# Stick-breaking heads in four steps: the next head's scan is queued behind the split of this head's turned weights

## The chip, the cores and the metric

The kernel runs on one core of a Trainium2 chip. The core has a matrix engine (TensorE, PE in the profile, with its weight loads shown apart as PEld), a vector engine (VectorE, DVE), an activation engine (ScalarE, ACT), GpSimd (POOL) and SyncE (SP), whose queue issues most of the transfers between the chip's memory and the core's own. Each engine works through its own instructions in the order in which they were written for it. The metric is the time of one execution on the device in microseconds (us), given as the median over the runs.

## The reference

The program is one block of a network on 512 tokens of width 1024: a normalisation and a projection, then two branches (stick-breaking attention with 16 heads of width 64, and a retention with 4 heads), a gated merge, and a feed-forward part. The change concerns only the stick-breaking branch and what is computed beside it:

```python
def stick_breaking_attention(q, k, v):
    ...
    for i in range(s_len // BLOCK):
        ...
        z = jnp.einsum('bhtd,bhsd->bhts', qb, kb).astype(jnp.float32) * scale
        ...
        mask = s_pos[None, :] < t_pos[:, None]
        log_1m_beta = jnp.where(mask, jax.nn.log_sigmoid(-z), 0.0)
        after = lax.cumsum(log_1m_beta, axis=3, reverse=True) - log_1m_beta
        log_a = jax.nn.log_sigmoid(z) + after
        a = jnp.where(mask, jnp.exp(log_a), 0.0)
        outs.append(jnp.einsum('bhts,bhsd->bhtd', a.astype(v.dtype), vb))
```

The merge that follows multiplies each branch by a gate, `sigmoid(br + b_branch)`, where `br` is a further part of the first projection. In the kernel these gates are computed in the same stretch of time as the heads.

## The kernel before

Everything is held transposed, features on the 128 partitions and tokens along the free axis. A float32 matrix product is made of three products of rounded parts: a value is split into a high part (a copy on ScalarE, L208) and a low part (the difference, on VectorE, L210), and one product of eight 128-row blocks is 24 matmuls of 128 x 512 (`gemm`). Weights come in by SP in tiles `raw` (three buffers) and are split into `whi` and `wlo` (four buffers each).

**One head.** `sb_front(h)` computes the scores of head h into three PSUM banks named `z` (8 matmuls, L614), takes two sigmoids of them on ScalarE (L622, eight instructions), and runs on VectorE a product scan from the right over each row (L625, two instructions) and a multiplication (L626, two instructions). What stands then in `b4` and `b1` are the attention weights, with queries on the partitions. `sb_back(h)` turns them: ten transposes on TensorE (L637) write three `z` banks, which are then split into high and low parts (L640 to L643: three copies on ScalarE, three differences on VectorE). With these it forms the output (eight matmuls into the bank `av`, L651), copies it out on ScalarE (L653), moves half of it to the other partitions by a transfer (L655) and adds (L656).

There are only three `z` banks (`BUFS`, L92). So the transposes of head h-1 write banks that the sigmoids of head h have just read, and the scores of head h+1 write banks that the splits of head h-1 have read.

**The order.** `heads(h)` at L1099 emits `sb_front(h)` and then `sb_back(h-1)`: on VectorE the scan of head h stands ahead of the differences of head h-1. Between heads the loop at L1111 places other products: after each even head up to 10 a pair of products `sb_qk(p)` for the queries and keys of two later heads, after each odd head one gate product (`mix(1)`), and after heads 13 and 15 four gate products each. A scheduler then moves the instructions of each engine against each other, by its own estimate of when each can start. It interleaves the transposes and output matmuls with the neighbouring product. In what it made of this, head h = 1, 3, 5, ... has two products ahead of it, and h = 2, 4, 6, ..., 12 has one. Heads 13 and 15 have less than one product between them and the head before.

`tc.issue_after(ins)` adds an ordering edge from the instructions of its block to `ins`, for those on the engine of `ins` only.

Of the kernel before, what the change touches and what calls it, by code (L numbers as in the profile page):

```python
# [117 lines left out]
def kernel(  # L118
# [19 lines left out]
    def nm(s):  # L138
        uid[0] += 1
        return f"{s}_{uid[0]}"  # L140
# [4 lines left out]
    def psa():  # L145
        return pspool.tile([P, S], F32, tag="av", bufs=BUFS["av"], name=nm("av"))

    def psz():
        return pspool.tile([P, S], F32, tag="z", bufs=BUFS["z"], name=nm("z"))

    def pair(tag):
        return apool.tile([P, 2, S], F32R, tag=tag, bufs=BUFS[tag], name=nm(tag))

    def tmp():
        return apool.tile([P, S], F32, tag="t", bufs=BUFS["t"], name=nm("t"))

    def otile():
        return apool.tile([P, S], F32, tag="o", bufs=BUFS["o"], name=nm("o"))
# [4 lines left out]
    def f(ap):  # L163
        return ap.bitcast(F32)
# [41 lines left out]
    def split(dst_hi, dst_lo, src, scale=1.0, eng=None):  # L206

        nc.scalar.activation(dst_hi, src, AF.Copy, scale=scale)  # L208
        if isinstance(scale, float) and scale == 1.0:
            return (eng or nc.vector).tensor_sub(dst_lo, src, f(dst_hi))  # L210
        return nc.vector.scalar_tensor_tensor(
            dst_lo, src, scale, f(dst_hi), op0=ALU.mult, op1=ALU.subtract
        )
# [15 lines left out]
    def mm(o, lhs, rhs, start, stop):  # L229
        return nc.tensor.matmul(o, lhs, rhs, start=start, stop=stop, skip_group_check=True).ins  # L230
# [99 lines left out]
    def sigmoid_tables():  # L330
        return tc.keep_in_program_order(nc.scalar.preload_act_table_set("sigmoid_and_others"))

    def ln_exp_tables():
        return tc.keep_in_program_order(
            nc.scalar.preload_act_table_set("natural_log_exp_and_others")
        )
# [222 lines left out]
    sbq, sbk, sbv = {}, {}, {}  # L559
# [16 lines left out]
    def sb_qk(p):  # L576
        qp, kp = ps(), ps()
        gemm(qp, weight(("sq", p)), hs)
        gemm(kp, weight(("sk", p)), hs)
        sb_qk_store(p, qp, kp)  # L580
# [27 lines left out]
    def sb_front(h):  # L608
        q, k = sbq[h], sbk[h]
        z = [psz(), psz(), psz()]  # L610
        for i, bank, c, _ in reversed(SEG):
            w = (i + 1) * P
            for n in range(2):
                head_pe[h] = mm(z[bank][:, c : c + w], q[:, n, i * P : (i + 1) * P], k[:, 0:w],  # L614
                                n == 0 and c == 0, n == 1)
        n4, n1, b4, b1 = stick_sets[h % 2]
        for segs in ((3,), (2, 0), (1,)):
            for (t4, t1), scale in (((n4, n1), -1.0), ((b4, b1), 1.0)):
                for i, bank, c, at in (SEG[i] for i in segs):
                    w = (i + 1) * P - 1  # L620
                    t = t1 if i == 1 else t4
                    nc.scalar.activation(t[:, at : at + w], z[bank][:, c : c + w], AF.Sigmoid, scale=scale)  # L622
        for n, b, d in ((n4, b4, diag), (n1, b1, diag[:, 640:896])):
            w = n.shape[-1]
            nc.vector.tensor_tensor_scan(n[:, ::-1], n[:, ::-1], d[:, ::-1], 0.0, op0=ALU.mult, op1=ALU.max)  # L625
            nc.vector.tensor_mul(b[:, 0 : w - 1], b[:, 0 : w - 1], n[:, 1:w])  # L626
        return b4, b1

    def sb_back(h, b4, b1):
        vt = sbv[h // 4]  # L630
        at = [psz(), psz(), psz()]
        for i, _, _, a in reversed(SEG):
            t = b1 if i == 1 else b4
            for j in range(i + 1):
                bank, c = TGEO[j]
                c += (i - j) * P
                nc.tensor.transpose(at[bank][:, c : c + P], t[:, a + j * P : a + (j + 1) * P], ident)  # L637
        avs = []
        for bank in range(3):
            w = TBANKW[bank]  # L640
            hl = pair("s")
            split(hl[:, 0, :w], hl[:, 1, :w], at[bank][:, :w])
            avs.append(hl)  # L643
        o = psa()
        r, hf = (h % 4) // 2, h % 2
        for j in (3, 2, 1, 0):
            bank, c = TGEO[j]
            w = S - j * P
            v = vt[j // 2][:, j % 2, r * 256 + hf * P : r * 256 + hf * P + P]
            for i in range(2):  # L650
                mm(o[:, j * P : S], v, avs[bank][:, i, c : c + w], j == 3 and i == 0, j == 0 and i == 1)  # L651
        u, u2 = tmp(), tmp()
        nc.scalar.activation(u, o, AF.Copy)  # L653
        own, oth = (slice(0, HD), slice(HD, P)) if hf == 0 else (slice(HD, P), slice(0, HD))
        nc.sync.dma_start(u2[own], u[oth])  # L655
        nc.vector.tensor_add(o_sb[h // 2][own], u[own], u2[own])  # L656
# [49 lines left out]
    def ret_v(h, first, between):  # L706
        vt = [pair("v") for _ in range(4)]
        for i in range(2):
            if i == 1:
                between()  # L710
            banks = first if i == 0 else [ps(), ps()]
            if i == 1:
                tok_proj(banks, [("rv", h, i, half) for half in range(2)])
            for b in range(4):
                c = slice(i * 256, (i + 1) * 256)
                split(vt[b][:, 0, c], vt[b][:, 1, c],
                      banks[b // 2][:, (b % 2) * 256 : (b % 2) * 256 + 256])
        return vt

    def ret_scores(h, qk):  # L720
        q1, q2, k1, k2 = qk
        z = [psz(), psz(), psz()]
        st = {}
        for j in (3, 2, 1, 0):
            bank, c, t0, w = GEO[j]
            js = slice(j * P, (j + 1) * P)
            for n, (q, k) in enumerate(((q1, k1), (q2, k2))):
                mm3(z[bank][:, c : c + w], k[:, 0, js], k[:, 1, js], q[:, 0, t0:S], q[:, 1, t0:S],
                    n == 0 and j != 2, n == 1)
        for j in (3, 2, 1, 0):  # L730
            bank, c, t0, w = GEO[j]
            if bank not in st:
                st[bank] = pair("s")
            hl = st[bank]
            split(hl[:, 0, c : c + w], hl[:, 1, c : c + w], z[bank][:, c : c + w],
                  gk[:, h * 4 + j : h * 4 + j + 1])
        for bank in (2, 1, 0):
            for i in range(2):
                causal(st[bank][:, i, :], bank)
        return st  # L740
# [317 lines left out]
    vt = ret_v(0, v_ps, lambda: st.update(ret_scores(0, qk)))  # L1058
# [6 lines left out]
    for h in range(3):  # L1065
# [3 lines left out]
        vt = lambda: [rvts[b] for b in range(4)]  # L1069
# [3 lines left out]
    act_table = sigmoid_tables()  # L1073
# [5 lines left out]
    def sb_v(g):  # L1079

        sbv[g] = [pair("v") for _ in PI]
        for n, vt in enumerate(sbv[g]):
            nc.sync.dma_start(f(vt), vspill[2 * (g - 2) + n])

    sbv.update({g: [vts[g, n] for n in PI] for g in PI})
    mixes = [(ret_mix, d) for d in range(8)] + [(sb_mix, d) for d in range(8)]

    def mix(n):
        for _ in range(n):
            fn, d = mixes.pop(0)  # L1090
            fn(d)
# [5 lines left out]
    fronts = {}  # L1097

    def heads(h):  # L1099
        with tc.issue_after(act_table.ins):  # L1100
            if h < 16:
                fronts[h] = sb_front(h)
            if h:
                if h % 8 == 1 and h > 8:
                    sb_v(2)
                    sb_v(3)
                if h % 2:
                    o_sb[h // 2] = otile()
                sb_back(h - 1, *fronts.pop(h - 1))

    for h in range(17):  # L1111
        heads(h)
        p = h // 2 + 2
        if h % 2 == 0 and p < 8:
            sb_qk(p)
        elif h % 2 and mixes:
            mix(1 if p < 8 else len(mixes) if h == 15 else 4)
    ln_exp_tables()
    acts = []
    for j in range(8):  # L1120
        hl = pair("q" if j < 4 else "s")
# [3 lines left out]
    for d in range(8):  # L1125
# [7 lines left out]
        hl = pair("h")  # L1133
        ins = split(hl[:, 0, :], hl[:, 1, :], t)
# [596 lines left out]
```

## Time and profile before

| | us |
|---|---|
| median of 3 runs | 1153.26 |
| lowest and highest run | 1152.96 and 1153.92 |
| profiled execution, its own time | 1152.75 |
| its span, first to last instruction | 1151.0 |

The profile is of that one execution. Its page shows for each engine the busy time and share of the span; other views show stretches of time (windows), single instructions in order of time (the timeline), and who waited for whom (waits). In these, a row's `[x <-ENGINE tile Lnnn]` says that the engine sat idle for x us before that row and what ended the idle time. `x7` at the end of a row means that seven equal instructions are merged into it. Instructions on one engine overlap at their ends, so rows start a little before the row above ends.

The heads lie between 478 and 710 us. The scores of head 1 start at 489.5 us and those of head 13 at 645.6 us.

### The profile page before, as it was taken

The numbers are of one execution on the slowest core, as the hardware profiler recorded it, in microseconds if no ns is written. First come the engines' busy times: TensorE is split into PE (matmuls) and PEld (weight loads), VectorE is DVE, ScalarE is ACT, GpSimd is POOL, SyncE is SP. The second block draws the span as 40 slices with busy tenths as digits, with TensorE's granted clock in tenths as the row PEclk, the third lists the DMA queues.
The fourth block names the chain that finished last, engine by engine and source line by source line (L and its number), as shares of the span: only waits on it lengthen the run. The fifth ranks groups of instructions, "written<-read, shape, count | busy, mean of one in ns | idle before, by whom it ended". The sixth has DMA issues, their size and how long they took to land. (4 is left out here: it accounts for less than half of the span.)

```text
span 1151.0 us, 16148 instructions
## 1 busy us (share of the span) xinstructions
PE 1119.5 (97%) x6196; PEld 965.2 (84%) x6196; DVE 839.5 (73%) x1181; ACT 554.4 (48%) x869; POOL 55.3 (5%) x94
## 2 busy tenths in 40 slices
PE   8999999999999999999999899999999999999996
PEld 7888888888888887877777678889999999999986
DVE  7997756959959867466666754776997776677656
ACT  5445345445445544355555544355744454454333
POOL 0000000111021110000000000000000000000000
PEclk9999999999999999999999999999999999999998
DMA  9724432766777576856565338872546654565322
GB/s 353 271 73 147 139 118 92 221 129 199 238 147 245 149 185 209 225 151 177 151 185 150 109 114 272 276 217 59 138 140 175 179 145 134 151 176 152 90 80 74
DMA packets 63437, 190.93 MB, mean 166 GB/s; under 512 B 7808, under 2 KB 9856, under 8 KB 63360
## 3 DMA queue, kind: packets, MB, share of 16 engines
q1 hardware_dynamic: 56048, 171.02, 46.6%
q0 software_dynamic: 6768, 18.35, 9.4%
q8 instruction: 49, 0.80, 0.3%
q10 hardware_dynamic: 544, 0.52, 0.1%
q14 instruction: 28, 0.23, 0.1%
HBM read 146.35 MB, written 16.78 MB: 142 GB/s over the span
## 5 line engine op out<-in xcount | busy, mean ns | idle before, releaser
L230 PE MATMUL ps<-h,whi 128*128 128x512 f32 (+1 forms) x1154 | 340.3, 376 | 0.2
L230 PEld LDWEIGHTS ps<-h,whi 128*128 128x128 f32 x1154 | 208.0, 189 | 35.1 <-ACT h L435 1.6
L230 PE MATMUL ps<-h,wlo 128*128 128x512 f32 (+1 forms) x577 | 214.6, 376 | 0.0
L210 DVE TENSOR_TENSOR wlo<-raw,whi 128x1024 fp32r<-128x1024 f32 (+1 forms) x106 | 127.3, 1201 | 99.3 <-ACT whi L208 96.6
L208 ACT ACTIVATE whi<-raw 128x1024 fp32r<-128x1024 f32 (+1 forms) x106 | 110.6, 1044 | 162.0 <-PE ps L230 108.5
L230 PE MATMUL ps<-s,whi 128*128 128x512 f32 x480 | 148.5, 390 | 0.0
L230 PEld LDWEIGHTS ps<-h,wlo 128*128 128x128 f32 x577 | 108.9, 189 | 17.4
L230 PE MATMUL z<-q,whi 128*128 128x256 f32 x504 | 106.8, 283 | 0.0
L230 PEld LDWEIGHTS ps<-s,whi 128*128 128x128 f32 x480 | 89.3, 188 | 18.5 <-DVE s L210 0.5
L871 DVE TENSOR_TENSOR wlo<-s,whi 128x1024 fp32r<-128x1024 f32 x46 | 56.2, 1225 | 54.7 <-ACT whi L867 54.7
L230 PE MATMUL ps<-s,wlo 128*128 128x512 f32 x240 | 93.4, 389 | 0.0
L230 PEld LDWEIGHTS z<-q,whi 128*128 128x128 f32 x504 | 84.9, 192 | 1.5
L867 ACT ACTIVATE whi<-s 128x1024 fp32r<-128x1024 f32 x47 | 49.7, 1057 | 58.6 <-PE ps L230 46.0
L230 PE MATMUL ps<-whi,h 128*128 128x512 f32 (+1 forms) x272 | 77.8, 365 | 0.0
L1172 DVE SCALAR_TENSOR_TENSOR o<-ps,mod,o 128x512 f32<-128x512 f32 (+1 forms) x63 | 42.4, 680 | 29.1 <-PE ps L230 29.1
L230 PEld LDWEIGHTS ps<-whi,h 128*128 128x128 f32 x272 | 49.2, 188 | 9.1 <-ACT t L1011 0.6
L230 PEld LDWEIGHTS ps<-s,wlo 128*128 128x128 f32 x240 | 45.1, 188 | 9.4
L867 ACT ACTIVATE whi<-raw 128x1024 fp32r<-128x1024 f32 x28 | 29.6, 1058 | 42.1 <-PE ps L230 40.3
L230 PE MATMUL ps<-wlo,h 128*128 128x512 f32 (+1 forms) x136 | 49.5, 364 | 0.0
L230 PE MATMUL ps<-q,whi 128*128 128x256 f32 (+1 forms) x224 | 49.2, 314 | 0.0
L230 PE MATMUL z<-qp,whi 128*128 128x256 f32 x168 | 47.2, 283 | 0.0
L230 PE MATMUL z<-q,wlo 128*128 128x256 f32 x168 | 46.4, 283 | 0.0
(318 smaller groups left out, 2105.1 us busy)
## 6 DMA issues: line engine op xcount, KB each, us to landing
raw<-wp SPq DMA_DIRECT2D x139, 512.0 KB, 4.1
araw<-wada SPq DMA_DIRECT2D x32, 512.0 KB, 4.0
araw<-wp SPq DMA_DIRECT2D x30, 512.0 KB, 4.7
s<-wp SPq DMA_DIRECT2D x24, 512.0 KB, 5.4
sraw<-wada SPq DMA_DIRECT2D x16, 512.0 KB, 7.4
q<-qp SPq DMA_DIRECT2D x32, 256.0 KB, 3.8
spill<-o POOLq DMA_DIRECT2D x24, 256.0 KB, 4.7
o<-xT SPq DMA_DIRECT2D x16, 256.0 KB, 4.2
```

Source lines behind the costliest of these rows:

```text
L208: nc.scalar.activation(dst_hi, src, AF.Copy, scale=scale)
L210: return (eng or nc.vector).tensor_sub(dst_lo, src, f(dst_hi))
L230: return nc.tensor.matmul(o, lhs, rhs, start=start, stop=stop, skip_group_check=True).ins
L867: nc.scalar.activation(hi, t, AF.Copy)
L871: nc.vector.tensor_sub(lo, t, f(hi))
L1172: return nc.vector.scalar_tensor_tensor(x1[d][:, hv], o[:, hv], mod[:, gcol + d : gcol + d + 1], x1[d][:, hv], op0=ALU.mult, op1=ALU.add,)
```

## The change

`sb_front` now ends with the sigmoids. The scan and the multiplication become `sb_scan`, the transposes and the split `sb_turn`, which also returns the last difference (`ins`), and the output matmuls with what follows become `sb_out`. `heads(h)` emits, in this order: scores and sigmoids of h, transposes and split of h-1, scan of h, output of h-1. The scan of h is put behind the last difference of h-1 on VectorE by `issue_after`. No instruction is added or removed, but for two runs of equal matmuls that now print as one row.

The loop now places two gate products after each of heads 12 to 15, in place of four after 13 and four after 15. Their sequence is unchanged.

```diff
                     nc.scalar.activation(t[:, at : at + w], z[bank][:, c : c + w], AF.Sigmoid, scale=scale)
+        return n4, n1, b4, b1
+
+    def sb_scan(n4, n1, b4, b1):
         for n, b, d in ((n4, b4, diag), (n1, b1, diag[:, 640:896])):
             w = n.shape[-1]
             nc.vector.tensor_tensor_scan(n[:, ::-1], n[:, ::-1], d[:, ::-1], 0.0, op0=ALU.mult, op1=ALU.max)
             nc.vector.tensor_mul(b[:, 0 : w - 1], b[:, 0 : w - 1], n[:, 1:w])
-        return b4, b1
-
-    def sb_back(h, b4, b1):
-        vt = sbv[h // 4]
+
+    def sb_turn(n4, n1, b4, b1):
         at = [psz(), psz(), psz()]
...
-            split(hl[:, 0, :w], hl[:, 1, :w], at[bank][:, :w])
+            ins = split(hl[:, 0, :w], hl[:, 1, :w], at[bank][:, :w])
             avs.append(hl)
+        return avs, ins
+
+    def sb_out(h, avs):
+        vt = sbv[h // 4]
         o = psa()
...
         with tc.issue_after(act_table.ins):
+            ins = act_table
             if h < 16:
                 fronts[h] = sb_front(h)
             if h:
                 if h % 8 == 1 and h > 8:
                     sb_v(2)
                     sb_v(3)
+                avs, ins = sb_turn(*fronts.pop(h - 1))
+            if h < 16:
+                with tc.issue_after(ins.ins):
+                    sb_scan(*fronts[h])
+            if h:
                 if h % 2:
                     o_sb[h // 2] = otile()
-                sb_back(h - 1, *fronts.pop(h - 1))
+                sb_out(h - 1, avs)
 
     for h in range(17):
         heads(h)
         p = h // 2 + 2
-        if h % 2 == 0 and p < 8:
+        if p > 7:
+            mix(min(2, len(mixes)))
+        elif h % 2:
+            mix(1)
+        else:
             sb_qk(p)
-        elif h % 2 and mixes:
-            mix(1 if p < 8 else len(mixes) if h == 15 else 4)
```

On VectorE, around head 1, the order before was the following. `qp` is the split of a key product, the SCALAR_TENSOR_TENSOR rows of L625 are the scans, and `s<-z` at L210 are the three differences of head 0's turned weights.

```order
L210 TENSOR_TENSOR qp_4279<-ps_4217,qp_4279 128x512
L625 SCALAR_TENSOR_TENSOR s_3955<-s_3955,table_3945 128x1024
L625 SCALAR_TENSOR_TENSOR t_3957<-t_3957,table_3945 128x256
L626 TENSOR_TENSOR s_3956<-s_3956,s_3955 128x1023
L626 TENSOR_TENSOR t_3957<-t_3957 128x255
L210 TENSOR_TENSOR s_4332<-z_4319,s_4332 128x512
L210 TENSOR_TENSOR s_4335<-z_4320,s_4335 128x512
L210 TENSOR_TENSOR s_4338<-z_4321,s_4338 128x256
L210 TENSOR_TENSOR wlo_4593<-raw_4590,whi_4592 128x1024
```

At the same place it now is:

```order
L210 TENSOR_TENSOR qp_4279<-ps_4217,qp_4279 128x512
L210 TENSOR_TENSOR s_4327<-z_4314,s_4327 128x512
L210 TENSOR_TENSOR s_4330<-z_4315,s_4330 128x512
L210 TENSOR_TENSOR s_4333<-z_4316,s_4333 128x256
L628 SCALAR_TENSOR_TENSOR s_3955<-s_3955,table_3945 128x1024
L628 SCALAR_TENSOR_TENSOR t_3957<-t_3957,table_3945 128x256
L629 TENSOR_TENSOR s_3956<-s_3956,s_3955 128x1023
L629 TENSOR_TENSOR t_3957<-t_3957 128x255
L210 TENSOR_TENSOR wlo_4593<-raw_4590,whi_4592 128x1024
```

The two scans and two multiplications have changed places with the three differences, and the rows before and behind them are the same.

On TensorE, in the product beside head 1 (`ps`), the output matmuls of head 0 (`av`) stood like this before, from the first of them on:

```order
L230 MATMUL av_4341<-s_4335,v_3845 128x128
L230 MATMUL ps_4355<-h_349,whi_4358 128x512
L230 MATMUL ps_4355<-h_349,wlo_4359 128x512
L230 MATMUL ps_4355<-h_396,whi_4358 128x512 x2
L230 MATMUL ps_4355<-h_396,wlo_4359 128x512
L230 MATMUL ps_4355<-h_443,whi_4358 128x512 x2
L230 MATMUL ps_4355<-h_443,wlo_4359 128x512
L230 MATMUL ps_4355<-h_491,whi_4358 128x512 x2
L230 MATMUL av_4341<-s_4335,v_3845 128x128
L230 MATMUL av_4341<-s_4338,v_3845 128x256 x2
L230 MATMUL av_4341<-s_4335,v_3719 128x384 x2
L230 MATMUL av_4341<-s_4332,v_3719 128x512 x2
```

They now stand like this:

```order
L230 MATMUL av_4341<-s_4330,v_3845 128x128
L230 MATMUL ps_4355<-h_349,whi_4358 128x512
L230 MATMUL ps_4355<-h_349,wlo_4359 128x512
L230 MATMUL ps_4355<-h_396,whi_4358 128x512 x2
L230 MATMUL av_4341<-s_4330,v_3845 128x128
L230 MATMUL av_4341<-s_4333,v_3845 128x256 x2
L230 MATMUL av_4341<-s_4330,v_3719 128x384 x2
L230 MATMUL av_4341<-s_4327,v_3719 128x512 x2
L230 MATMUL ps_4355<-h_396,wlo_4359 128x512
```

Four matmuls of the product stand between the first output matmul and the other seven, where ten stood before. In heads 2, 4, ..., 12 and in 13 to 15 it is three.

## The prediction

> **What bounds the kernel now.** I read the page's first part, then windows over the stretch with the heads, then the waits in it, and last the timeline of single heads.
>
> ```profile
> PE 1119.5 (97%) x6196; PEld 965.2 (84%) x6196; DVE 839.5 (73%) x1181; ACT 554.4 (48%) x869; POOL 55.3 (5%) x94
> 489.00:640.00 151.00, 140.15 (x689) 109.29 (x688) 102.71 (x123) 77.65 (x171) 0.00 (x0) 1.00 0.61 161
> 640.00:690.00 50.00, 45.01 (x224) 35.34 (x224) 33.51 (x40) 25.79 (x58) 0.00 (x0) 1.00 0.35 114
> 690.00:712.00 22.00, 22.00 (x105) 18.18 (x104) 7.60 (x10) 10.08 (x15) 0.00 (x0) 1.00 0.77 253
> 712.00:1151.00 439.00, 429.47 (x2917) 399.27 (x2915) 321.26 (x419) 213.34 (x278) 19.75 (x23) 0.99 0.51 148
> ```
>
> TensorE bounds the kernel. A window row gives the stretch, its length, the busy time of PE, PEld, DVE, ACT and POOL, the granted clock, the share of the DMA engines and GB/s. Among the heads, 489 to 690 us, PE is idle for 10.85 + 4.99 us; after them hardly at all before the end. VectorE has room there (102.71 of 151 us), so its speed is not the limit, though its order may be. What TensorE stood for, in the waits of weight loads and matmuls between 440 and 712 us:
>
> ```profile
> PEld av L230 <- DVE s L210: 17.2, 13, 1.6
> PEld z L637 <- ACT s L622: 11.6, 28, 0.6
> PEld z L230 <- DVE s L210: 3.1, 2, 1.6
> PE av L230 <- DVE s L210: 11.7, 13, 1.1
> PE z L230 <- DVE s L210: 2.2, 2, 1.1
> ```
>
> (us in total, times, longest.) Fifteen times, once for each head from 1 to 15, TensorE waited for the differences of the turned weights (s, L210): 13 times with the output matmuls, twice with the next scores, which need the z banks back. The 11.6 us are transposes waiting until the sigmoids have left the z banks; the change leaves that as it is. Head 1 in the timeline (start, length, row):
>
> ```profile
> 492.67 2.29 DVE L625 TENSOR_TENSOR_SCAN s<-s,table 128x1024 f32<-128x1024 f32 x1 [0.24 <-ACT s L622]
> 496.57 0.42 DVE L626 TENSOR_TENSOR t<-t 128x255 f32<-128x255 f32 x1
> 496.91 1.61 DVE L210 TENSOR_TENSOR s<-z,s 128x512 fp32r<-128x512 f32 x3
> 493.47 1.45 ACT L208 ACTIVATE s<-z 128x512 fp32r<-128x512 f32 x3
> 496.77 0.62 PE L230 MATMUL ps<-h,whi 128*128 128x512 f32 x2
> 498.24 1.54 PE L230 MATMUL av<-s,v 128*128 128x128 f32 x7 [0.85 <-DVE s L210]
> 498.24 1.10 PEld L230 LDWEIGHTS av<-s,v 128*128 128x128 f32 x7 [1.28 <-DVE s L210]
> 499.62 0.40 PE L230 MATMUL ps<-h,wlo 128*128 128x512 f32 x1
> ```
>
> ScalarE begins the copies of the turned weights at 493.47, but VectorE is in head 1's scan and multiplications from 492.67 to 496.99, so head 0's differences begin only at 496.91. TensorE has used up its ten filling matmuls by 497.4 and stands.
>
> **How long one such stand is.** The matmul row says 0.85 us, the weight load row 1.28. The same seven output matmuls without a wait, in head 16:
>
> ```profile
> 707.07 0.39 PE L230 MATMUL ps<-q,whi 128*128 128x512 f32 x1
> 708.45 0.39 PE L230 MATMUL ps<-q,whi 128*128 128x512 f32 x1
> ```
>
> From the start of the matmul ahead of them to that of the one behind them it is 1.38 us here. In head 1 the matmul ahead starts at 496.77 + (0.62 - 0.39) = 497.00, the one behind at 499.62: 2.62 us. The loss is 1.24 us, which is the 1.28 of PEld less the 0.04 that a load idles anyway (a matmul every 0.23 us against a load of 0.19). So I take the PEld rows: 17.2 + 3.1 - 15 x 0.04 = **19.7 us**. By the PE rows it would be 11.7 + 2.2 = 13.9 us; I keep that as the other bound.
>
> The Trainium skill, "Perfetto Trace Analysis", section "Tensor Engine Instruction (MATMUL, LD_WEIGHTS)", says that a matmul's reported end is worked out from its size and not observed. The two intervals agree with it: they give 1.24 us where the matmul rows leave 0.85. By the matmul rows the sum would be 13.9 us, by the load rows 19.7.
>
> **The change part by part.** Nothing is computed more or less; TensorE, VectorE and ScalarE get the same instructions and SP the same transfers.
>
> *The differences ahead of the scan* (15 heads). They can begin when the first copy is done; the second copy releases the first output matmul. The copies of head 1 by tile (shortest, median and longest in ns, the short one being half as wide), and the loads of the first output matmul and of the product's third or fourth behind it in heads 1 and 2:
>
> ```profile
> L208 ACT ACTIVATE s<-z x3: 500/686/702, 493.5 to 494.4; 128x512 fp32r<-128x512 f32 x2, 128x256 fp32r<-128x256 f32 x1
> 494.70 0.19 PEld L230 LDWEIGHTS av<-s,v 128*128 128x128 f32 x1 [0.28 <-ACT s L208]
> 495.62 0.19 PEld L230 LDWEIGHTS ps<-h,wlo 128*128 128x128 f32 x1
> 505.79 0.19 PEld L230 LDWEIGHTS av<-s,v 128*128 128x128 f32 x1 [0.16 <-ACT s L208]
> 506.48 0.19 PEld L230 LDWEIGHTS ps<-h,wlo 128*128 128x128 f32 x1
> ```
>
> The first copy of head 1 then ends at 493.47 + 0.69 = 494.16. Three differences take 1.61 us, about 0.68 for a wide one with the next starting 0.6 behind it: the second ends near 495.5, the third near 495.8. The seven output matmuls need the second and, three matmuls later, the third. In the new order four filling matmuls precede them, so their load would come where the load at 495.62 is now: nothing to wait for, and the whole 1.24 us is gone. In head 2, and like it in heads 4 to 12 and 13 to 15, only three precede them. Their load could come at 506.48, and the second difference ends, by the same steps from the copies' start at 504.57 (below), near 506.6: a new wait of about 0.14 us, nine times, **1.3 us** back. Its bounds are 0 and 0.4 (a difference later by one filling matmul), 0 to 3.6 us.
>
> *The scan behind the differences.* It starts at about 495.8 in place of 492.67 and takes 492.67 to 496.99, 4.3 us: it ends at 500.1. Behind it on VectorE stand the low part of the next weights, a gate's product and the add of the last output; who waits for the scan is the transpose of the next head.
>
> ```profile
> 500.55 1.38 PE L230 MATMUL z<-q,q 128*128 128x512 f32 x8
> 503.17 0.20 PEld L637 LDWEIGHTS z<-con,s 128*128 128x128 f32 x2 [0.47 <-ACT s L622]
> 501.60 1.23 DVE L210 TENSOR_TENSOR wlo<-raw,whi 128x1024 fp32r<-128x1024 f32 x1 [3.08 <-ACT whi L208]
> 502.75 0.68 DVE L826 TENSOR_TENSOR g<-g 128x512 f32<-128x512 f32 x1
> 503.35 0.68 DVE L656 TENSOR_TENSOR o<-t,t 64x512 f32<-64x512 f32 x1
> 504.57 1.44 ACT L208 ACTIVATE s<-z 128x512 fp32r<-128x512 f32 x3
> ```
>
> Head 2's scores now start at 500.55 and its first transpose at 503.17, held by the sigmoids. Both come 1.24 us earlier when head 1's stand is gone: 499.3 and 501.9. The scan is done 1.8 us before that. This is the tight place, since only one product lies between heads 1 and 2, and likewise up to 11 and 12; elsewhere a further product of 24 x 0.23 = 5.5 us lies between. The next weights' low part waited 3.08 us for ScalarE, so at 500.1 it is still not late; the gate's product and the add follow by 502.8, before the next copies (504.57 - 1.24 = 503.3). Cost: 0, and without this margin the transposes of six heads would wait.
>
> *The gate products two by two.* Heads 13 and 15 lose the crowding, in which the next scores waited for the z banks (the 3.1 us above) and then the output matmuls again:
>
> ```profile
> 655.38 1.10 PEld L230 LDWEIGHTS av<-s,v 128*128 128x128 f32 x7 [1.55 <-DVE s L210]
> ```
>
> These four stands are already in the 19.7 us. Their waits for sigmoids stay as in the other heads. In the same order each gate's write is queued on SP next to the load of later weights; two weight loads pass two q copies each.
>
> ```profile
> raw<-wp SPq DMA_DIRECT2D x28, 512.0 KB, 4.1
> ```
>
> A load lands 4.1 us after its issue. There are three raw buffers, and a product lasts 5.5 us, so a load is issued two products or more ahead and I cost this at nothing. If the cover were gone, a product would wait for its weights, at most 4.1 us at one place.
>
> **The sum.** 19.7 - 1.3 = 18.4 us off the profiled execution's 1152.75 us: 1134.3. The median of the runs is 0.5 us above the profiled one, so I say 1134.5 us. What follows the heads runs with TensorE busy and keeps its own pace, so it only starts earlier.
>
> **The rivals.**
>
> *Only the idle time of the matmul rows comes back*, with the new wait at its full bound: 13.9 - 3.6 = 10.3 us, 1142.5; with the small one 12.6 us, 1140. For it: TensorE's own rows have no more idle time to give at these waits. Against it: the two intervals above. Chance 0.13.
>
> *More comes back*, because shorter heads also pull the sigmoids forward and the transposes wait less. All of the differences' waits and a quarter of the 11.6 us: 19.7 + 2.9 = 22.6, 1130.5. Against it: ScalarE starts the sigmoids behind the weights' copy, which waits for the same product's end, so both move together. Chance 0.07.
>
> *The stand moves to the z banks.* If three banks for scores and turned weights were the limit, the 20.3 us would turn up as longer waits of the transposes for sigmoids, and the time would stay: 1152.7. Against it: the output matmuls read splits in memory and not banks, and only the 3.1 us of the scores are a bank given back late. Chance 0.03. The Trainium skill, "Perfetto Trace Analysis", section "Optimization Strategy", would have it so: it says that equal bubbles along a stretch can mean too little SBUF or PSUM for the next tile. The 11.6 us of transposes fit that, the 17.2 us don't.
>
> *Slower: the scan becomes the bound of the heads.* Transposes, differences, scan and the next head's transposes are now one chain around the loop; up to now the scan stood outside the wait for the transposes. If the scan also fell behind the next weights' low part, the gate's product and the add (502.8 by the working above), it would end at 507.1 and the transposes at 501.9 would wait 5.2 us in six heads: 31 us, less 18.4: 1165. It decides from a delay of 1.8 us on, and makes the kernel slower from 1.8 + 18.4 / 6 = 4.9 us. For it: such a chain repeats in every head. Against it: the scan's rows stand straight behind the differences. Chance 0.04.
>
> **Chances and range.** The forecast, 16 to 20 us off, has 0.73. The range runs from 1131, between the forecast and the case of more, to 1140.5, which takes in the matmul rows with the small new wait. A measurement of this kernel can tell about 0.2% (2.3 us) from no change; faster by more has 0.73 + 0.13 + 0.07 = 0.93, no change 0.03, slower 0.04.
>
> **What would show it.** In the changed profile the wait of output matmuls for DVE s falls from 17.2 us to under 2, that of scores for DVE s is gone, and that of transposes for sigmoids stays within 10 to 13 us. No transpose waits for the multiplication behind the scan (s, L629). In the timeline each head's differences start 0.7 us behind the start of its copies, the scan follows without a gap, and heads 13 and 15 look like head 3. PE's busy share among the heads rises to 96% or more. I am wrong if transposes wait for VectorE, if the output matmuls wait again by more than 0.4 us a head, or if a product of the later stages waits for weights.

## The result and the profile after

| | time, median | runs | ratio to before, 95% interval |
|---|---|---|---|
| before | 1153.11 us | 1152.96 to 1153.92, 4 | |
| changed | 1138.19 us | 1136.24 to 1140.9, 4 | 0.9871 [0.985, 0.9892] |
| forecast | 1134.5 us, range 1131 to 1140.5 | | |

The kernel is 1.3% faster. The profiled execution of the changed kernel took 1136.24 us, its span 1134.2. First the windows over the heads, with the columns that the prediction names:

```profile
478.00:640.00 162.00, 160.52 (x801) 129.10 (x801) 120.26 (x142) 89.42 (x196) 0.00 (x0) 1.00 0.65 176
640.00:690.00 50.00, 49.83 (x249) 40.04 (x248) 30.63 (x37) 28.14 (x57) 0.00 (x0) 1.00 0.48 160
690.00:712.00 22.00, 21.14 (x94) 17.10 (x93) 14.86 (x27) 7.36 (x10) 0.00 (x0) 1.00 0.89 300
```

In the windows 489 to 640 and 640 to 690 us PE was idle for 10.85 + 4.99 us before; now it is 1.48 + 0.17 us, although the first window here begins 11 us earlier. What TensorE's weight loads waited for between 440 and 712 us:

```profile
PEld z L638 <- ACT s L622: 12.8, 30, 0.6
PEld av L230 <- ACT s L208: 3.5, 16, 0.4
PEld av L230 <- DVE s L210: 1.7, 9, 0.2
PEld ps L230 <- ACT s L208: 1.3, 1, 1.3
PEld ps L230 <- DVE s L210: 0.2, 1, 0.2
```

The 17.2 us of output matmuls waiting for the differences are 1.7, in nine places of 0.19; the scores' 3.1 us are gone. The transposes still wait for the sigmoids: 12.8 us, against 12.5 before (the 11.6 us that the prediction shows, and 0.9 us for the second sigmoid tile, `t`). Head 1 in the timeline:

```profile
494.15 1.46 ACT L208 ACTIVATE s<-z 128x512 fp32r<-128x512 f32 x3
494.87 1.62 DVE L210 TENSOR_TENSOR s<-z,s 128x512 fp32r<-128x512 f32 x3 [1.77 <-ACT s L208]
496.41 2.28 DVE L628 TENSOR_TENSOR_SCAN s<-s,table 128x1024 f32<-128x1024 f32 x1
500.30 0.42 DVE L629 TENSOR_TENSOR t<-t 128x255 f32<-128x255 f32 x1
502.61 0.20 PEld L638 LDWEIGHTS z<-con,s 128*128 128x128 f32 x2 [0.49 <-ACT s L622]
506.06 1.10 PEld L230 LDWEIGHTS av<-s,v 128*128 128x128 f32 x7 [0.19 <-DVE s L210]
```

The differences start 0.72 us behind the copies, the scan follows without a gap, its last multiplication ends at 500.72, and the next transposes come 1.89 us after that. Nothing waits for the scan.

To see where the time went, one can cut the span at instructions that both kernels have. The rows give, for a group of matmuls, the first and the last start. Before:

```profile
L230 PE MATMUL z<-q,whi x504: 277/283/283, 815.7 to 1110.8; 128*128 128x256 f32 x168
L637 PE MATMUL z<-con,s x128: 270/273/332, 492.1 to 704.5; 128*128 128x128 f32 x128
```

And changed:

```profile
L230 PE MATMUL z<-q,whi x504: 277/283/283, 798.8 to 1094.0; 128*128 128x256 f32 x168
L638 PE MATMUL z<-con,s x128: 270/272/329, 492.8 to 686.6; 128*128 128x128 f32 x128
```

`z<-con,s` are the transposes of the heads, `z<-q,whi` belongs to the later stages. From the first to the last transpose TensorE does the same 963 matmuls in both kernels, so the two lengths can be compared.

| stretch of the profiled execution | before | changed | difference |
|---|---|---|---|
| up to the first transpose of a head | 492.1 | 492.8 | +0.7 |
| first to last transpose: the heads | 212.4 | 193.8 | -18.6 |
| to the first `z<-q,whi` | 111.2 | 112.2 | +1.0 |
| to the end of the span | 335.3 | 335.4 | +0.1 |
| outside the span | 1.75 | 2.04 | +0.3 |
| sum | 1152.75 | 1136.24 | -16.5 |

So the heads gave what was forecast (18.4 us), and 2 us came back elsewhere. The +1.0 has its place in the timeline: the last head's halves change partitions by a transfer on SP (t to t), and the first product behind the heads waits for the sum:

```profile
690.79 0.33 SPq L203 DMA_DIRECT2D araw<-wada  x1
691.36 0.47 SPq L660 DMA_DIRECT2D t<-t  x1
696.21 0.69 DVE L661 TENSOR_TENSOR o<-t,t 64x512 f32<-64x512 f32 x1 [4.99 <-DMA t<-t]
697.67 0.30 PEld L230 LDWEIGHTS ps<-s,whi 128*128 128x128 f32 x2 [1.28 <-ACT s L208]
```

The add starts 4.85 us after the transfer is issued, which stands 0.57 us behind a 512 KB load. Before, that load was 0.93 us ahead, the add followed after 3.83 us, and the product's wait was 0.2 us. The second and the third experiment come back to this.

### The profile page after: what moved, and what is told of

Its sections match the earlier page's. It is cut to its first block, busy times and chain, and to the rows that moved or that the text cites. A ratio compares the mean times of both kernels' runs of the same rounds, so it can differ in the third digit from the quotient of the medians.

```text
span 1134.2 us, 16143 instructions
## 1 busy us (share of the span) xinstructions
PE 1115.5 (98%) x6196; PEld 965.4 (85%) x6196; DVE 839.7 (74%) x1181; ACT 554.6 (49%) x869; POOL 55.3 (5%) x94
## 4 chain that ended last, share of the span: by engine, by line
PE 82%; DVE 7%; DMA 4%; ACT 4%; issue 2%; SPq 0%; DVEq 0%; ACTq 0%
PE ps L230 63%; PE z L230 14%; PE av L230 3%; DMA araw<-wada 3%; PE z L638 2%; DVE araw L258 2%; ACT s L622 1%; DVE wlo L876 1%; DVE wlo L210 1%; ACT g L825 1%; DVE t L783 0%; DMA t<-t 0%; PE z L787 0%; DMA o<-xT 0%; DVE s L211 0%
## 5 line engine op out<-in xcount | busy, mean ns | idle before, releaser
L210 DVE TENSOR_TENSOR wlo<-raw,whi 128x1024 fp32r<-128x1024 f32 (+1 forms) x106 | 127.3, 1202 | 68.3 <-ACT whi L208 67.7
L230 PEld LDWEIGHTS ps<-h,wlo 128*128 128x128 f32 x577 | 108.9, 189 | 17.2
L210 DVE TENSOR_TENSOR s<-z,s 128x512 fp32r<-128x512 f32 (+1 forms) x60 | 33.6, 613 | 28.8 <-ACT s L208 28.8
```

## The experiments

They ran in three groups, each with runs of the kernel before beside it: the first four below (median of before 1153.91 us), the next four (1154.49) and the last two (1153.47).

### The changed kernel once more, unaltered

> The changed kernel once more, unaltered, for its spread. Both theories: 1136 to 1141 us. If the last head's transfer between partitions (t<-t, 4.8 us to land in the first profile) is what varies, the wait of the product for the last output's high part (ps<-s,whi for ACT s, 1.3 us before) differs in this profile and the span differs by about the same amount. If the clock is what varies, that wait stays at 1.3 us and the granted clock goes with the time (0.994 at 1140.9 us against 0.997 at 1136.2 us).

Measured: 1137.45 us (1135.91 to 1140.89), ratio 0.9856 [0.9838, 0.9873]. The same kernel spreads over 5 us. The slowest and the fastest of these four executions had the same mean granted clock (0.997), so the clock alone does not explain the spread; it may still have a part in it, since the slowest of the first four (1140.9 us) had 0.994. In this profile the heads took 193.8 us again, and the exchange's wait was 1.8 us in place of 1.3. That is most of the 0.7 us between the two profiled executions, as the first of the two theories has it, but neither of them was a long one. The profile of a long execution is in the run with the loads held back, below.

### Only the gate products two by two

```diff
@@ before, loop over the heads
-        if h % 2 == 0 and p < 8:
+        if p > 7:
+            mix(min(2, len(mixes)))
+        elif h % 2:
+            mix(1)
+        else:
             sb_qk(p)
-        elif h % 2 and mixes:
-            mix(1 if p < 8 else len(mixes) if h == 15 else 4)
```

> The kernel before, with only the gate products placed two by two. Theory (the gain is the order of scan and differences): still fifteen stands of 1.2 us or more, 1151 to 1154 us. Rival (spreading the products brings a good part of it, since heads 13 and 15 lost 6.2 us to differences): 1146 to 1149 us.

Measured: 1154.0 us (11 runs), ratio 1.0001 [0.9992, 1.0009]. Output matmuls waited for the differences 15 times, 20.1 us in all: the scores' two waits of before have become waits of outputs. Moving products about gives nothing while the differences are late. Its last exchange is slower than that of the kernel before: the 512 KB load stands 0.42 us ahead of it, the add follows after 4.38 us, and the first product behind the heads waits 1.1 us. So that loss does not need the shorter heads.

### Only the four steps, with the gate products where they were

The same two places the other way round: the changed kernel with the old rule for the products.

> The four steps and the edge, with the gate products placed as before (four after head 13, four after 15). Theory: heads 1 to 12 gain as in the changed kernel; in heads 13 and 15, where less than one product lies between, the scan ends 8.0 us after the head's first transpose and the next transposes are reached some 6 us after it, so they wait 1.5 to 2 us for VectorE: 1140 to 1144 us. Rival (the placement of the products does not matter): 1137 to 1139 us, as the changed kernel.

Measured: 1137.04 us (4 runs), ratio 0.985 [0.9837, 0.9863]. A miss: I had expected 1140 to 1144, since heads 13 and 15, where the next scores crowd in, should wait for the scan. They do; the rows of the weight load and of the matmul in the timeline of this run:

```profile
635.58 0.54 PEld L638 LDWEIGHTS z<-con,s 128*128 128x128 f32 x5 [1.68 <-ACT s L622]
635.61 0.75 PE L638 MATMUL z<-con,s 128*128 128x128 f32 x5 [1.27 <-DVE s L629]
```

The load's row names the sigmoids, the matmul's the multiplication behind the scan. But this wait of 1.68 us comes in place of the head's usual 0.49 + 0.40 for sigmoids, not on top of them. From first to last transpose the heads take 195.6 us, 1.8 more than in the changed kernel for two such places. In the time this does not show: the new place of the products is worth at most 2 us, and the four steps are the gain. The load stands 0.93 us ahead of the last exchange here, as in the kernel before, but the add follows after 4.36 us and the product waits 0.8 us.

### The four steps without the edge that holds the scan

```diff
             if h < 16:
-                with tc.issue_after(ins.ins):
-                    sb_scan(*fronts[h])
+                sb_scan(*fronts[h])
```

> The changed kernel without the explicit edge that puts the scan behind the last difference. The scheduler then leaves the differences behind the scans and one or two multiplications, with eight (odd heads) or four (even heads) matmuls between the first output matmul and the others. Theory: each head stands 1.2 to 1.4 us again, 15 times, 1151 to 1156 us. Rival (that the program emits turned weights ahead of the scan is enough): 1137 to 1141 us.

Measured: 1154.68 us (12 runs), ratio 1.0004 [0.9995, 1.0014]. Output matmuls waited 20.3 us again, as the first row says. The others are VectorE's in head 1 of this run's timeline:

```profile
PEld av L230 <- DVE s L210: 20.3, 15, 1.4
...
492.77 2.29 DVE L628 TENSOR_TENSOR_SCAN s<-s,table 128x1024 f32<-128x1024 f32 x1 [0.24 <-ACT s L622]
...
495.56 1.20 DVE L629 TENSOR_TENSOR s<-s,s 128x1023 f32<-128x1023 f32 x1
496.68 1.61 DVE L210 TENSOR_TENSOR s<-z,s 128x512 fp32r<-128x512 f32 x3
```

Written in four steps, the scan still stands ahead of the differences on VectorE, whose operands come later. Without the edge the new order of the text does nothing; with its two lines comes the whole gain of 1.3%.

### How much room the scan has

One and then two operations of 128x1024 that leave the values as they are, ahead of each scan (the diff shows two):

```diff
     def sb_scan(n4, n1, b4, b1):
+        for _ in range(2):
+            nc.vector.tensor_tensor(n4, n4, n4, op=ALU.max)
```

> The changed kernel with one more VectorE operation of 128x1024 (a maximum of a value with itself, about 1.15 us) ahead of each scan. In head 1 the scan's multiplication ends 1.89 us ahead of the next transposes in the changed kernel. Theory (this margin is real): 1.15 us less of it costs nothing in the short heads, 0 to 1 us in all, 1137 to 1138.5 us, and no transpose waits for the multiplication. Rival (the margin is already used up by work behind the scan, the next weights' low part or the add): 3 us or more, over 1140.

> As the run with one more operation, with two (about 2.3 us) ahead of each scan. Theory: that is 0.4 us more than the margin of 1.89 us, so the transposes of the six short heads wait for the scan, and VectorE's work in such a head (10.55 us) is then longer than the head itself (9.85), so that the differences come some 0.7 us late as well: 1.1 us in each of six heads, 1141 to 1146 us. Rival (the scan has room in every head, since something else is later): 1137 to 1138.5.

Measured: with one, 1137.3 us, ratio 0.9863 [0.984, 0.9886], and the heads nearly keep their length (194.5 us, 0.7 more). With two, 1143.09 us, ratio 0.9903 [0.9881, 0.9924], the heads 198.0 us. Both times are as expected, but the second only in part for the reason given: the heads grew by 4.2 us and not by 6.6, and in this profile the wait for the last exchange, 3.9 us, adds to it. With two, the waits of matmuls among the heads have a row that the changed kernel has not, for the multiplication behind the scan:

```profile
PE z L640 <- DVE s L631: 3.7, 5, 0.8
```

The margin of 1.89 us is real: an operation of 1.22 us fits into it and two do not. So the prediction's slower rival, in which the scan becomes the bound, is a mechanism that exists; heads 13 and 15 of the run with the gate products in their old place show it too. In head 1 the changed kernel stays 1.89 us short of it.

### The loads held behind the last exchange

```diff
-        nc.sync.dma_start(u2[own], u[oth])
+        exchange[0] = nc.sync.dma_start(u2[own], u[oth])
...
-            ada_after(ins)
+            with tc.issue_after(exchange[0].ins):
+                ada_after(ins)
...
-        nc.sync.dma_start(x1[d], xT[d * P : (d + 1) * P, :])
+        with tc.issue_after(exchange[0].ins):
+            nc.sync.dma_start(x1[d], xT[d * P : (d + 1) * P, :])
```

> The changed kernel with one thing altered: the 512 KB load (araw) and the loads of x that stood on SP just ahead of the last head's exchange of halves (t to t) are queued behind it. Theory: the time that the heads save beyond what TensorE's own waits account for went into this exchange, whose 4.9 to 5.4 us follow from the load queued 0.4 to 0.6 us ahead of it. Then the exchange lands in under 4 us, the wait of the first product behind the heads falls from 1.3 to 1.8 us to about 0.2, and the time is 1135.8 to 1136.5 us. Rival: the load only turns up later and the exchange takes as long without it; the wait stays above 1 us and the time at 1137 to 1138.5.

Measured: 1137.48 us (1134.21 to 1139.99), ratio 0.9857 [0.9833, 0.9881]: as a time, no change, and above the 1135.8 to 1136.5 us that I expected. The mechanism is as I said; in the timeline of this run:

```profile
695.95 0.47 SPq L662 DMA_DIRECT2D t<-t  x1
...
697.63 0.85 SPq L203 DMA_DIRECT2D araw<-wada  x2
...
698.23 0.69 DVE L663 TENSOR_TENSOR o<-t,t 64x512 f32<-64x512 f32 x1 [2.42 <-DMA t<-t]
```

The add starts 2.28 us after the issue, not 4.85, and the product's wait falls from 1.3 or 1.8 to 0.3 us. From the last transpose to the first `z<-q,whi` it is 111.3 us in place of 112.2. Which of the loads held back does it, the 512 KB one or those of x, the run does not tell. But this profiled execution took 1139.99 us, and it shows one place where the spread can lie: its heads begin at 497.3 us, 4.5 us later than in the changed kernel's profile. Windows ahead of the heads in it, the last of them a part of the first:

```profile
240.00:320.00 80.00, 76.94 (x346) 63.68 (x345) 62.89 (x113) 34.99 (x50) 5.47 (x10) 0.98 0.58 185
320.00:400.00 80.00, 78.99 (x360) 64.88 (x359) 62.23 (x98) 39.36 (x58) 10.14 (x17) 1.00 0.62 171
294.60:298.01 3.41, 3.41 (x16) 3.21 (x14) 2.34 (x3) 2.35 (x4) 0.00 (x0) 0.50 1.00 388
```

and its waits of weight loads between 230 and 400 us:

```profile
PEld z L789 <- DVE t L785: 3.4, 3, 2.3
PEld ps L230 <- DVE wlo L878: 1.6, 1, 1.6
```

PE lost 4.07 us in the two long windows, where the changed kernel's profile lost 1.66 (78.53 and 79.81 of 80 us busy) and the kernel before 0.22 (79.78 and 80.00). The clock of 0.98 in the first is the mean over one short spell: for 3.41 us it was granted at 0.50, beginning 1.1 us after the longest of these waits (2.3 us) had ended. Half of 3.41 us is 1.7 us of work; with the 2.4 us that PE lost more, that is 4.1 of the 4.5 us. The first of these waits goes from 0.5 to 3.4 us over the profiles of this study, ahead of every edit. An effect of 1 us behind the heads can't be told from it by whole times.

### The sigmoids earlier

What is left is 12.8 us of transposes waiting for sigmoids. On ScalarE a copy of the next weights (whi, 1.06 us) runs shortly ahead of the sigmoids. I held it behind the copies of the turned weights, the last of which is `copied[0]` here:

```diff
                 avs, ins = sb_turn(*fronts.pop(h - 1))
+                turned[h - 1] = copied[0]
...
+        with tc.issue_after(turned[h - 2].ins if h > 1 else act_table.ins):
-        if p > 7:
+            if p > 7:
...
```

> The changed kernel with ScalarE's copies of the next weights (whi, 1.06 us each) held behind the copies of the turned weights, where in the changed kernel they stand straight ahead of the sigmoids. Theory: what is left, 12.8 us of transposes waiting for sigmoids in 30 places, is ScalarE being in such a copy when the scores are ready; with the copy gone the sigmoids start up to 0.8 us earlier, the waits fall to 2 to 5 us, and the time to 1128 to 1132 us. Rival: the low part of those weights now comes behind the scan on VectorE and the product waits for it, and gives the gain back: 1136 to 1141.

Measured: 1138.98 us (4 runs), ratio 0.9876 [0.9857, 0.9894]: the theory fell, and the rival has the time but not the cause, since no product waited for the low part of its weights. The weight loads in head 1 of this kernel, from the timeline:

```profile
497.61 1.45 PEld L232 LDWEIGHTS z<-q,q 128*128 128x128 f32 x8
498.98 0.30 PEld L232 LDWEIGHTS ps<-h,whi 128*128 128x128 f32 x2
499.74 0.20 PEld L640 LDWEIGHTS z<-con,s 128*128 128x128 f32 x2 [0.46 <-ACT s L624]
...
500.84 0.31 PEld L640 LDWEIGHTS z<-con,s 128*128 128x128 f32 x3 [0.41 <-ACT s L624]
```

The transposes come 2.13 us after the scores, where it was 2.86 (502.61 against scores at 499.75): the sigmoids are 0.7 us earlier. But the scheduler, which counts on that, puts two filling matmuls ahead of the transposes in place of five, and the wait is 0.46 us as it was 0.49. The matmuls that it took out run later, and TensorE does the same work with nearly the same gaps. In this profile its heads even took 195.5 us, 1.7 more; 0.7 of that are three matmuls of the product that now come behind the first transpose.

### More filling, at fixed places

So the gap is a matter of the number of filling matmuls. Here each step of a head is hung on a counted matmul of the product:

```diff
+    weave, due = [], (7, 9, 10, 11, 14, 18)
...
     def mm3(o, lh, ll, rh, rl, start, stop):
-        mm(o, lh, rh, start, False)
-        mm(o, lh, rl, False, False)
-        mm(o, ll, rh, False, stop)
+        for lhs, rhs, first, last in ((lh, rh, start, False), (lh, rl, False, False), (ll, rh, False, stop)):
+            ins = mm(o, lhs, rhs, first, last)
+            for run in weave:
+                run(ins)
...
+            count[0] += 1
+            while count[1] < 6 and (ins is None or count[0] == due[count[1]]):
+                count[1] += 1
+                with tc.issue_after(ins or act_table.ins):
+                    next(gen)
```

`gen` yields after the transposes into each of the three banks, after the differences and the scan, after the first output matmul and after the rest. For that the transposes are also written bank by bank, which the lines shown leave out.

> The changed kernel with one thing altered, TensorE's order among the heads: the product's matmuls that fill the waits are put at fixed places, 7 ahead of the first four transposes (4 or 5 before), 2 ahead of the next four, 1 ahead of the last two, 4 ahead of the first output matmul and 4 ahead of the other seven (3 and 3 or 4 before). The order on ScalarE and VectorE is that of the changed kernel. Theory: the run that started the sigmoids 0.7 us earlier gained nothing at these waits because the scheduler put 2 filling matmuls in place of 5 there, so what is left, 12.8 + 3.5 + 1.7 = 18.0 us of waits, is a matter of how much is filled in and not of ScalarE's or VectorE's speed; the waits fall to 2 to 6 us and the time to 1121 to 1127 us. Rival 1 (VectorE becomes the bound: a short head is then 8.6 us long and holds 8.3 to 8.5 us of VectorE work, and the scan's margin goes from 1.89 to about 0.4 us): 3 to 8 us come back as waits for the scan or for the differences, 1128 to 1133. Rival 2 (the chain through ScalarE's sigmoids and copies sets the pace and the fillers only move the waits): 1136 to 1139.

Measured: 1127.95 us (1126.87 to 1130.07, 5 runs), ratio 0.9773 [0.9759, 0.9786], 10 us below the changed kernel, and the fastest version of this study beside the next. The waits of weight loads among the heads are as the theory has them, 1.8 + 1.6 = 3.4 us in place of 18.0 (the 2.7 and the 0.2 us belong to the product behind the last head, which waits for the exchange and the split of its sum):

```profile
PEld ps L230 <- ACT s L208: 2.7, 1, 2.7
PEld z L643 <- ACT s L625: 1.8, 9, 0.2
PEld av L230 <- ACT s L208: 1.6, 4, 0.4
PEld ps L230 <- DVE s L210: 0.2, 1, 0.2
```

No wait for VectorE is left among the heads, so neither rival holds. Yet the time is 1 us above the range that I gave, just short of the 1128 where the first rival's range begins. The waits fell by 14.6 us, the heads only from 193.8 to 185.6 (491.8 to 677.4 by the rows of the transposes). And 0.7 us of that are three matmuls of the product that now run ahead of the first transpose, so 7.5 us are saved. What the rest of the 10 us is, the profiles do not tell: the profiled execution is the slowest of the five, and behind its heads it lost 3 us against the changed kernel (115.2 us in place of 112.2). Its stand for the exchange is 1.4 us longer, and behind it the clock was granted at half:

```profile
689.92 0.73 PE L230 MATMUL ps<-s,whi 128*128 128x512 f32 x2 [2.25 <-ACT s L208]
...
691.04:694.45 3.41, 3.41 (x10) 2.63 (x9) 1.69 (x3) 1.75 (x2) 0.00 (x0) 0.50 0.63 178
```

The second row is a window. Matmuls start every 0.42 us in it, in place of 0.23, which costs the other 1.7 us. The other four executions had a clock of 0.997 or 0.998.

A short head in the timeline of the changed kernel, from the scores of one head to those of the next, and on to the transposes:

```profile
490.21 1.37 PE L230 MATMUL z<-q,q 128*128 128x512 f32 x8
...
499.98 1.37 PE L230 MATMUL z<-q,q 128*128 128x512 f32 x8
...
501.93 0.62 PE L230 MATMUL ps<-h,whi 128*128 128x512 f32 x2
502.61 0.44 PE L638 MATMUL z<-con,s 128*128 128x128 f32 x2
```

The same in the kernel with more filling, and the transposes' weight load:

```profile
488.87 1.37 PE L230 MATMUL z<-q,q 128*128 128x512 f32 x8
...
498.07 1.38 PE L230 MATMUL z<-q,q 128*128 128x512 f32 x8
...
500.72 0.40 PE L230 MATMUL ps<-h,whi 128*128 128x512 f32 x1
500.96 0.38 PE L643 MATMUL z<-con,s 128*128 128x128 f32 x2
...
500.73 0.38 PEld L643 LDWEIGHTS z<-con,s 128*128 128x128 f32 x2
```

The head is 9.77 us in the one and 9.20 in the other, 0.57 less for the same matmuls, where the weight loads between these two scores had waited 0.62 + 0.18 + 0.28 = 1.08. The transposes behind the second scores show why. Without a wait their load starts at 500.73 and its matmul at 500.96: the load runs 0.23 us ahead, under the matmul before it. With the wait, of 0.49 us here, load and matmul start together at 502.61; from the start of the matmul ahead, 501.93 + (0.62 - 0.39) = 502.16, that is 0.45 us, against 0.24 without it. So 0.49 us of the load's idle time cost 0.21: the first 0.2 us or so only use up the lead. The Trainium skill, "TensorE: Matmul & The Clock Gate", section "Step-by-step: what each phase is for", says that weight loads are pulled ahead of running matmuls while these stay in order; the 0.23 us of lead agree with it.

### The filling and the held loads together

> The filling of the run before together with the loads held behind the last head's exchange. Theory: both are independent, and the exchange's wait of 1 to 4 us falls to 0.3: 1 to 2 us below the filling alone, 1119.5 to 1126 us. Rival: the loads held back come late for the sums behind the heads, and the time is that of the filling alone or above.

Measured: 1128.06 us (4 runs), ratio 0.9774 [0.976, 0.9787]: 2 us above the range, and the time that the rival gives. Its cause does not show: no wait of TensorE behind the heads is longer than 0.5 us. In the profile the exchange's add again starts 2.28 us after its issue and not 5.17, and from the last transpose to the first `z<-q,whi` it is 112.1 us against 115.2. But this execution reached the heads 1.9 us later, and the medians are the same. Of the 3.1 us between the two stretches, 1.7 are the spell at half clock, which this execution did not have. Whether holding the loads back is worth the 1 to 3 us that the stretch shows, these times can't tell.

## Why the prediction was right, point by point

**The time.** The kernel is faster and the median lies inside the range, but by the number alone this does not settle the mechanism. The drop was 14.9 us by the first medians (16.5 in the next group), where 16 to 20 had been forecast, and 1138.19 us is nearer to the rival's 1140, by which only the matmul rows' time comes back, than to 1134.5. What decides between them is the length of the heads, which fell by 18.6 us.

**The bound and the stand.** Right. TensorE stood for the differences behind the scan; taking the scan out of their way took the stands away, and leaving the edge out brought back all 20.3 us of them.

**19.7 us by the load rows, not 13.9 by the matmul rows.** Right for these stands. The heads became 18.6 us shorter. Nine new short waits lie in that. Where such a wait is gone, from the matmul ahead of seven outputs to the one behind them is 1.39 us (504.49 to 505.88 in the run with more filling), and with it 1.51 (505.92 to 507.43 in the changed kernel): 0.12 us each, 1.1 in all, and 18.6 + 1.1 is the 19.7. But the rule that I drew, a load's wait less 0.04 us, holds only for a long stand ahead of several short matmuls. At the short waits that the filling took away it gives far more than there was: 14.6 us in 42 places, 12.9 us by the rule, against 7.5 us of shorter heads. The run with more filling was expected too fast by that step.

**A new wait of 0.14 us, nine times, 1.3 us.** Nine times 0.19 us, at a cost of 0.12 us each, 1.1 us: the term holds, if not to the last digit (the prediction's own steps give a wait of about 0.1 us).

**The scan's margin of 1.8 us.** 1.89 us, and the two runs with longer VectorE work bracket it.

**The gate products two by two, nothing on their own.** Right: alone they gave 0.9992 to 1.0009. With the four steps their place in heads 13 and 15 saves 1.8 us of the heads in the profile, which the times can't tell; so 16.8 of the 18.6 us are the four steps alone.

**"What follows the heads runs with TensorE busy and keeps its own pace, so it only starts earlier."** This is the step that failed, by 1.0 us in the profile: the product behind the heads waits for the last head's exchange, and that transfer now takes 4.85 us to its reader in place of 3.83. With the loads ahead of it held back it took 2.28 us, and the stretch was 0.9 us shorter, so it is the loads that make it long. That it became longer because the 512 KB load stands closer is not shown: with that load 0.93 us ahead, as before, the run of the four steps alone had 4.36 us. I had read the wait behind the heads before as nothing, since it was 0.2 us, without asking what its transfer was queued behind.

**"The median of the runs is 0.5 us above the profiled one."** The forecast was 1134.3 us for the profiled execution, which took 1136.24, and 1134.5 for the median, which was 1138.19. Of the 1.9 us in the profile, 1.0 is the exchange, 0.7 lies ahead of the heads, 0.1 behind the later stages' begin, 0.3 outside the span, and the heads were 0.2 better. The other 2.0 us are the spread: an offset of one profile to three runs, which I carried over, is no property of the kernel, and three runs within 1 us were too few to see a spread of 5 us. The kernel before has it too: its 23 runs beside the first group went from 1152.22 to 1157.15 us.

**The rivals.** That only the matmul rows' time comes back would have left the heads 10 to 12.6 us shorter; they were 18.6. That more comes back needed shorter waits for sigmoids; they went from 12.5 to 12.8 us. That the stand moves to the z banks did not happen. Behind that rival stood a sentence of the Trainium skill, "Perfetto Trace Analysis", section "Optimization Strategy", by which even bubbles can mean too little SBUF or PSUM; the 12.8 us of transposes seemed to fit it. The trace doesn't agree: with the same three banks the filling took them to 1.8 us. That the scan becomes the bound takes more delay than one added operation of 1.22 us and less than two, and the changed kernel has none; with the gate products in their old place it happened in two heads.

## What to carry to other kernels

Where an engine runs its queue in order, look for a long operation that nobody waits for yet, standing ahead of a short one that another engine waits for; writing it behind is not enough where a scheduler orders by readiness, an edge is. Price an idle gap by the interval between the starts of the same instructions with and without it: the matmul rows said 99% busy while 7.5 us were still to be had, and the load rows said 18. And before speeding up what a gap waits for, see whether the order would just move the filling work out of the gap; a counted number of matmuls in it made the kernel 10 us faster where an earlier producer gave nothing.

## What the runs showed of the hardware that was not expected

A transfer between partitions of SBUF (t to t, issued on SP) was followed by its reader after 2.28 us where no large load stood close ahead of it, in both runs with the loads held back. With a 512 KB load ahead of it in the same queue it took longer, but not by a clear rule: 3.83 and 4.36 us with the load issued 0.93 us ahead, 4.85 us with 0.57, and 4.38 to 5.76 us in the seven profiles with 0.42 or 0.43.

The first 0.2 us of a weight load's wait cost nothing at the transposes, since without a wait the load runs 0.23 us ahead of its matmul.

The clock fell to half for a short time after a stand of TensorE. In three profiles the longest stand, 2.25, 2.64 and 3.87 us from the start of one matmul to that of the next (the loads held back, more filling, two added operations), was followed 1.1 to 1.4 us after its end by 3.41 us at 0.50. No stand of up to 2.21 us in the twelve profiles was, leaving out the first 25 us and the end of the span. So a wait of about 2.3 us or more cost some 1.7 us beyond itself here; that the stand is what brings the clock down is read from these three cases and was not tested.
